# Phase boundaries of a two-layer trunk: single tiles transposed, norms by half rows, other places for the second-half sums

## The chip, the cores and the metric

The kernel runs on one core of one Trainium2 chip. The metric is device time in microseconds (us) of one execution. The kernel before takes 2263.08 us, the median of 3 runs (2262.11 to 2267.9).

## The reference, cut to what matters

The kernel computes two layers of a trunk over 640 tokens of width 1024: 512 sample tokens and 128 prompt tokens, in fp32. Each layer has three sublayers: a gated FFN of inner width 2816, a token mixer (RG-LRU scans in layer 0, window pooling in layer 1) and a second FFN. Each of the three does the same around its core:

```python
h = _modulate(_rmsnorm(x, norm_g[l, 0]), sh1, sc1)
x = x + 0.5 * g1 * _rmsnorm(_swiglu(h, ffn_w1[l, 0], ffn_w3[l, 0], ffn_w2[l, 0]), norm_g[l, 1])
```

So a sublayer needs 1/rms of x per token, a scaling and a shift per column, the core, 1/rms of its result y, and a product with a gate row. The shifts, scales and gates come from a matmul of the conditioning vector with a large weight (the modulation).

## The kernel before, in words

The tokens lie in five tiles of 128: tiles 0 to 3 are the sample, tile 4 the prompt. A row tile `y[t]` or `x` is 128 tokens by 1024. Matmul operands are fp32 numbers split into a high and a low part (`split`: ScalarE copies the high part, L207, VectorE subtracts for the low part, L208), with three matmuls for each product. Weights are split in the same way from a loaded tile `raw` (L136 on ScalarE, L137 on VectorE) and handed out by a generator that makes them ahead as far as a fixed number of buffers allows (`done`, `ahead`).

There are six phases (layer, sublayer): (0,0) FFN, (0,1) RG-LRU, (0,2) FFN, (1,0) FFN, (1,1) pooling, (1,2) FFN. The first products of an FFN go by a seven-product scheme on the token halves of 320 columns: the operands `A11`, `A12` need the first 320 tokens (tiles 0, 1 and half of 2), while `S1` to `S4` and `A22` need the second half too, through sums (`h_sums`, L410 to L413: four VectorE operations and five splits). `ffn_start` (L608) runs four products with `A11` and four with `A12` (96 matmuls of 320 columns, L472), and `seven_rest` then takes `S2`, `S3`, `S1`, `A22` and `S4` (12 matmuls each).

A phase ends in `final` (L575). For each tile it runs the last 24 matmuls of 512 columns (L553), adds them to y in two halves (L561), and then:

- `c_res`: sum of squares of y on ScalarE over 1024 columns (L349), addition of the epsilon on VectorE (L350), power -1/2 on POOL (L352), y times 1/rms times gate row G in one VectorE operation (L376), addition to x (L377).
- `c_next`: the same norm for x (L349, L350, L352), a scaled copy into y on ScalarE (L382), and a store of x to memory (L383).
- `c_h`: for tiles 0 and 1, 2 and 3, and 4 alone, transposes on TensorE (L430), scale and shift on VectorE (L447) and ScalarE (L449), and the splits or sums.

Pairs mean that tiles 0 and 1 are transposed after tile 1's norm, 2 and 3 after tile 3's:

```python
PAIRS = {1: (0, 1), 3: (2, 3), 4: (4,)}
```

Pooling has `pool_start` (L872: mix products, L897) and `pool_rest` (L930), which runs `pool_box` (L907, matmuls L918) for a tile, then `c_res` and `c_next` of it. RG-LRU has `rg_start` (L796) and `rg_rest`.

The modulation is a generator too (`mod_gen`, L262): each step loads 512 KB into one of two buffers `mw` and runs four small matmuls. The two buffers are shared with the x tiles of the final. `mod_step(n)` places n steps at given points of the program, and `mod_until` runs what is left. The gate rows G are made by L304 (TensorE) and L307 (ScalarE) into a single buffer.

The program is handed to a scheduler that fixes the order on each engine from the order of the code and from its own estimates; the order in which an engine works through its queue doesn't change at run time.

## Time and profile before

| | |
|---|---|
| median of 3 runs | 2263.08 us |
| the profiled execution | 2265.16 us, of which 2263.4 are its span |
| TensorE (PE) | 2114.6 us busy, 93% of the span, 13015 matmuls |
| VectorE (DVE) | 1688.3 us, 75% |
| ScalarE (ACT) | 979.9 us, 43% |
| POOL | 78.2 us, 3% |
| memory traffic | 260.40 MB read, 15.74 MB written, 122 GB/s over the span |

The profile names engines PE, PEld (weight loads of PE, beside PE), DVE, ACT, POOL and SP (the queue that issues most DMAs). `L472` is line 472 of the kernel. PEclk is the share of full speed that TensorE's clock was granted; 0.5 is its lower level of 1.2 GHz, 1.0 is 2.4 GHz. Idle time of an engine is listed with what ended it.

### The profile page before, as it was taken

How to read it: one execution, taken by the hardware profiler on the slowest of the kernel's cores; microseconds unless marked ns; L12 is line 12 of the kernel's file. 1: busy time of each engine (PE TensorE's matmuls, PEld its weight loads, DVE VectorE, ACT ScalarE, POOL GpSimd, SP SyncE). 2: the span in 40 equal slices, each digit the busy share in tenths (PEclk: the TensorE clock that was granted, in tenths of full speed). 3: DMA queues.
4: the chain of work that ended last, by engine and by line, in shares of the span. 5: the costliest groups of instructions: out<-in, count | busy, mean ns of one | idle time of the engine just before them, and what ended most of it. 6: DMA issues, size and time to landing. Idle time of an engine off the chain costs nothing.

```text
span 2263.4 us, 32357 instructions
## 1 busy us (share of the span) xinstructions
PE 2114.6 (93%) x13015; PEld 1894.6 (84%) x13015; DVE 1688.3 (75%) x2604; ACT 979.9 (43%) x1555; POOL 78.2 (3%) x107
## 2 busy tenths in 40 slices
PE   6899999997998699999998899999998499999998
PEld 4788889986897588899997788898997389999996
DVE  5967777765988786777776867777777587787875
ACT  5443333355856553333335543332337454333332
POOL 0000000000211100000000000000001000000000
PEclk7999999998999799999999899999999699999999
DMA  8424322235433443322223543344235452222222
GB/s 277 165 98 140 131 103 94 75 112 167 136 112 112 149 173 131 130 98 72 92 75 124 197 149 131 115 147 149 75 103 175 155 174 94 75 91 70 83 75 93
DMA packets 72710, 278.23 MB, mean 123 GB/s; under 512 B 7392, under 2 KB 15600, under 8 KB 61296
## 3 DMA queue, kind: packets, MB, share of 16 engines
q1 hardware_dynamic: 72528, 276.16, 35.2%
q8 instruction: 102, 1.67, 0.3%
q14 instruction: 48, 0.39, 0.1%
q0 software_dynamic: 32, 0.01, 0.0%
HBM read 260.40 MB, written 15.74 MB: 122 GB/s over the span
## 4 chain that ended last, share of the span: by engine, by line
PE 75%; DVE 10%; ACT 6%; DMA 5%; issue 2%; POOL 1%; SPq 1%; POOLq 0%; ACTq 0%; DVEq 0%
PE q L472 43%; PE b L553 24%; PE m L262 2%; PE b L472 2%; DMA mw<-in_mod_w_dram 2%; DMA raw<-in_w_dram 2%; PE q L481 2%; DVE mw L377 2%; POOL st L352 1%; DVE yacc L376 1%; DVE wp L177 1%; DVE h L776 1%; ACT h L738 1%; DVE h L208 1%; DVE wp L137 1%
## 5 line engine op out<-in xcount | busy, mean ns | idle before, releaser
L472 PE MATMUL q<-h,wp 128*128 128x320 f32 x6912 | 1049.7, 312 | 6.0 <-DVE c L504 2.6
L472 PEld LDWEIGHTS q<-h,wp 128*128 128x128 f32 x6912 | 1024.1, 189 | 35.4 <-issue 15.2
L553 PE MATMUL b<-wp,g 128*128 128x512 f32 x2880 | 670.6, 392 | 2.8 <-DVE g L208 2.0
L553 PEld LDWEIGHTS b<-wp,g 128*128 128x128 f32 x2880 | 537.7, 188 | 120.9 <-issue 6.2
L136 ACT ACTIVATE wp<-raw 128x512 fp32r<-128x512 f32 x440 | 267.6, 628 | 636.5 <-PE b L553 294.3
L137 DVE TENSOR_TENSOR wp<-raw,wp 128x512 fp32r<-128x512 f32 x440 | 298.1, 689 | 107.0 <-ACT wp L136 106.2
L561 DVE TENSOR_TENSOR yacc<-yacc,b 128x512 f32<-128x512 f32 x380 | 258.3, 685 | 119.4 <-PE b L553 117.3
L177 DVE TENSOR_TENSOR wp<-raw,wp 128x1024 fp32r<-128x1024 f32 x118 | 144.2, 1223 | 69.7 <-PE q L472 59.5
L174 ACT ACTIVATE wp<-raw 128x1024 fp32r<-128x1024 f32 x94 | 99.6, 1061 | 151.2 <-PE q L472 143.3
L136 ACT ACTIVATE wp<-T 128x512 fp32r<-128x512 f32 x176 | 109.3, 627 | 104.2 <-PE q L472 103.3
L137 DVE TENSOR_TENSOR wp<-T,wp 128x512 fp32r<-128x512 f32 x176 | 118.0, 689 | 14.4 <-ACT wp L136 14.2
L150 DVE TENSOR_TENSOR T<-raw 128x1024 f32<-128x1024 f32 x88 | 107.7, 1224 | 26.7 <-DMA raw<-in_w_dram 25.4
L481 PE MATMUL q<-h,wp 128*128 128x320 f32 x768 | 123.6, 316 | 2.2 <-DVE wp L177 2.2
L481 PEld LDWEIGHTS q<-h,wp 128*128 128x128 f32 x768 | 116.2, 191 | 9.9 <-issue 4.9
L262 PE MATMUL m<-mw,csil 128*32 128x256 f32 x1024 | 85.3, 402 | 23.2 <-DMA mw<-in_mod_w_dram 22.3
L430 PE MATMUL q<-cols,yacc 128*128 128x128 f32 x200 | 38.1, 351 | 67.9 <-ACT yacc L382 67.6
L352 POOL TENSOR_TENSOR st<-st,mhalf 128x1 f32<-128x1 f32 x60 | 43.6, 726 | 1562.1 <-DVE st L350 1553.8
L430 PEld LDWEIGHTS q<-cols,yacc 128*128 128x128 f32 x200 | 30.3, 181 | 78.4 <-ACT yacc L382 78.0
L207 ACT ACTIVATE g<-c 128x1280 fp32r<-128x1280 f32 x44 | 56.2, 1277 | 71.8 <-DVE c L537 71.5
L472 PE MATMUL b<-h,wp 128*128 128x320 f32 x480 | 74.9, 312 | 2.5 <-DVE c L497 1.3
L472 PEld LDWEIGHTS b<-h,wp 128*128 128x128 f32 x480 | 71.1, 188 | 6.1 <-issue 2.5
L208 DVE TENSOR_TENSOR g<-c,g 128x1280 fp32r<-128x1280 f32 x44 | 65.5, 1488 | 10.0 <-ACT g L207 9.7
(184 smaller groups left out, 1584.0 us busy)
## 6 DMA issues: line engine op xcount, KB each, us to landing
raw<-in_w_dram SPq DMA_DIRECT2D x88, 1024.0 KB, 4.8
mw<-in_mod_w_dram SPq DMA_DIRECT2D x130, 512.0 KB, 4.3
raw<-in_w_dram SPq DMA_DIRECT2D x88, 512.0 KB, 4.6
...
wp<-in_mod_w_dram SPq DMA_DIRECT2D x8, 512.0 KB, 10.4
```

The lines of the kernel that those rows point to most:

```text
L136: nc.scalar.activation(w[:, 0:512], src, AF.Copy)
L137: V.tensor_sub(w[:, 512:D], src, w[:, 0:512].bitcast(F32))
L150: V.tensor_sub(T, raw[:, 512:1536], raw[:, 0:1024])
L174: nc.scalar.activation(wh, r, AF.Copy)
L177: V.tensor_sub(wl, r, wh.bitcast(F32))
L208: self.nc.vector.tensor_sub(lo, src, hi.bitcast(F32))
L262: nc.tensor.matmul(ps[32 * j:32 * j + 32, 0:256], self.csil[:, k, :], w[:, j * 256:(j + 1) * 256], start=(k == 0), stop=(k == KC - 1), til ...
L430: nc.tensor.transpose(pt[:, q * w + i * P:q * w + (i + 1) * P], self.y[t][:, (j * n + q) * P:(j * n + q + 1) * P], self.col("ident"))
L472: self.nc.tensor.matmul(out, a, b[:, k], start=(start and not onto and k == first and n == 0), stop=(stop and k == last and n == 2), skip_ ...
L481: self.nc.tensor.matmul(out, a[:, sl], b[k // 2][:, k % 2, cols], start=(n == 0), stop=(n == 3 * KC - 1))
L553: nc.tensor.matmul(pb, a[:, ts_], b[:, ns], start=(c == 0), stop=(c == 3 * len(fl) - 1))
L561: nc.vector.tensor_add(y, y, pb)
```

## The change

1. **Norms by half rows.** `square` takes 512 columns and adds into one of two columns of a statistic; one VectorE operation (L347) adds the two and the epsilon; the power on POOL stays. y times G runs by halves (L379) without 1/rms; then x = y times 1/rms plus x, by halves (L387). The copies to y are by halves too (L399).
2. **`close`**, shared by `final` and pooling, runs product, half norm, product, half norm, and transposes tile t-2 while tile t is under way. Tiles are transposed one at a time into two banks (L476), and tiles 3 and 4 not in `close` at all: `ffn_start` and `rg_start` place them between the first products of the next phase, `pool_start` after the mixes of tiles 0 to 2.
3. **`h_sums`** is a generator: S2 first, the other sums later, with second-half columns in tiles of their own.
4. **Weights and modulation.** `room` keeps six weight buffers free at the start of an FFN and gives them back one per product. `mod_step(5)` and `mod_step(4)` go from `ffn_start`, `mod_step(9)` from `rg_start`.
5. RG-LRU's state transpose moves behind the final, and the second column block's first product starts earlier.

```diff
--- before.py
+++ after.py
...
-        nc.scalar.activation(junk, src, AF.Square, scale=1.0 / 32.0, accum_out=ms)
-        nc.vector.tensor_scalar(ms, ms, EPS, None, op0=ALU.add)
...
+        nc.vector.scalar_tensor_tensor(ms[:, 0:1], ms[:, 0:1], EPS, ms[:, 1:2], op0=ALU.add, op1=ALU.add)
...
+    def square(self, junk, src, ms, n):
+        self.nc.scalar.activation(junk, src, AF.Square, scale=1.0 / 32.0, accum_out=ms[:, n:n + 1])
...
-        rs = self.rstd(y)
...
-        nc.vector.scalar_tensor_tensor(y, y, rs, self.G[(l, s)][:, v], op0=ALU.mult, op1=ALU.mult)
-        nc.vector.tensor_add(x, x, y)
...
+    def res_half(self, t, n, l, s):
+        y = self.y[t][:, n * 512:(n + 1) * 512]
+        self.square(self.t("mhl", [P, 512], BF16), y, self.ms, n)
+        self.nc.vector.tensor_mul(y, y, self.G[(l, s)][:, v, n * 512:(n + 1) * 512])
+    def res_close(self, t):
+        x, y = self.xt[t], self.y[t]
+        rs = self.rstd(self.ms)
+        for n in range(2):
+            ns = slice(n * 512, (n + 1) * 512)
+            self.nc.vector.scalar_tensor_tensor(x[:, ns], y[:, ns], rs, x[:, ns], op0=ALU.mult, op1=ALU.add)
+    def c_next(self, t):
+        x, y = self.xt.pop(t), self.y[t]
+        ms = self.t("st", [P, 2])
+        for n in range(2):
+            ns = slice(n * 512, (n + 1) * 512)
+            self.square(y[:, ns], x[:, ns], ms, n)
+        rs = self.rstd(ms)
+        for n in range(2):
+            ns = slice(n * 512, (n + 1) * 512)
+            self.nc.scalar.activation(y[:, ns], x[:, ns], AF.Copy, scale=rs)
...
+    def h_sums(self, ks, cols, second):
         V = self.nc.vector
+        f21, f22, s1, s2 = second
+        f11, f12 = (x[:, ks, cols] for x in self.F[0])
         V.tensor_add(s1, f21, f22)
+        V.tensor_sub(s2, s1, f11)
+        self.h_put("S2", ks, cols, s2)
+        yield
+        V.tensor_sub(f11, f11, f21)
+        self.h_put("S3", ks, cols, f11)
+        self.h_put("S1", ks, cols, s1)
+        self.h_put("A22", ks, cols, f22)
+        V.tensor_sub(f12, f12, s2)
+        self.h_put("S4", ks, cols, f12)
...
-    def c_h(self, tiles, l, s, plain):
+    def c_t(self, t, l, s, plain, tag="q"):
...
+                if w < P:
+                    tmp = self.t("yacc", [P, D]).rearrange("p (n k t) -> p n k t", n=4, k=HK)
+                    second = [tmp[:, n] for n in range(4)]
+                else:
+                    if t == 3:
+                        self.f2 = [self.t("g", [P, 2 * TOK])[:, 0:D].rearrange("p (k t) -> p k t", k=HK) for _ in range(4)]
+                    o = (t - 3) * P
+                    second = [x[:, :, o:o + P] for x in self.f2]
+                parts.append((slice(a - t * P, P), lambda kk: second[kk // HK][:, kk % HK]))
+                self.sums[t] = self.h_sums(slice(0, HK), slice(a - HT, b - HT), second)
...
+        self.room = max(0, self.room - self.room_step)
+        self.done(1, self.room)
...
+    def close(self, product, l, s, nxt):
         if nxt:
             (self.new_plain if nxt[2] else self.new_h)()
+        self.sums = {}
         for t in range(NT):
+            self.res_open(t)
+            for n in range(2):
+                product(t, n)
+                self.res_half(t, n, l, s)
+            self.res_close(t)
             if nxt:
+                self.c_next(t)
+                if t >= 2:
+                    self.c_t(t - 2, *nxt)
             else:
                 self.store(t)
         self.x_home = self.spill
+        self.g_busy = False
+    def final(self, fl, l, s, nxt, start_next):
+        ws = [self.pair() for _ in fl]
+        self.close(lambda t, n: self.mmB(t, n, fl, ws, False), l, s, nxt)
         self.g.clear()
         if not nxt:
             return
+        start_next(nxt, 2 * len(fl))
...
-    def ffn_start(self, nxt):
+    def ffn_start(self, nxt, used):
         self.mod_allow(self.phase_mods[nxt[0:2]])
         self.ffn_open()
-        for m in range(4):
+        self.room, self.room_step = 6, 0
+        self.done(used, self.room)
+        copy = lambda m: self.nc.scalar.activation(self.s1[m], self.c11[m], AF.Copy)
+        for m in range(2):
             self.prod(self.c11[m], "A11")
-            self.nc.scalar.activation(self.s1[m], self.c11[m], AF.Copy)
-        self.mod_step(5)
-        for m in range(4):
+            copy(m)
+        self.c_t(3, *nxt, tag="b")
+        for m in range(2, 4):
+            self.prod(self.c11[m], "A11")
+            copy(m)
+        for t in (2, 3):
+            next(self.sums[t])
+        for m in range(2):
             self.prod(self.c11[m], "A12", onto=True)
-        self.mod_step(4)
-        self.ahead()
+        self.c_t(4, *nxt, tag="b")
+        next(self.sums[4])
+        for m in range(2, 4):
+            self.prod(self.c11[m], "A12", onto=True)
+        for t in (2, 3, 4):
+            next(self.sums[t], None)
+        self.room_step = 1
...
+        self.done(used, 5)
+        w = [self.pair(), self.pair()]
+        self.rg_xr(0, w[0], 0)
+        self.c_t(3, *nxt, tag="b")
+        self.rg_xr(1, w[1], 0)
+        self.c_t(4, *nxt, tag="b")
         self.rx = [self.t("h", [P, 2 * XW]) for _ in range(6)] + [self.t("c", [P, 2 * XW]) for _ in range(2)]
-        w = self.pair()
-        self.rg_xr(0, w, 0)
-        self.mod_step(9)
-        self.rg_xr(0, w, 1)
+        self.rg_xr(0, w[0], 1)
         self.done(2, 2)
         self.rg_conv(0)
         self.rg_xsplit(0)
+        self.rg_xr(1, w[1], 1)
+        self.done(2, 4)
...
+        self.final((4, 5, 6, 7), l, s, nxt, start_next)
         pt = self.p("m")
         self.nc.tensor.transpose(pt[0:16, 0:P], self.nst, self.col("ident"))
         so = self.t("mrow", [P, P])[0:16]
         self.nc.vector.tensor_copy(so, pt[0:16, 0:P])
         self.nc.gpsimd.dma_start(self.io["out_st"], so)
-        self.final((4, 5, 6, 7), l, s, nxt, start_next)
...
+        for pr in range(2):
+            for t in range(3):
+                mix(t, pr)
+        for t in range(3, NT):
+            self.c_t(t, *nxt)
...
-        self.new_h()
-        for t in range(NT):
-            self.pool_box(t)
-            self.c_res(t, l, s)
-            self.c_next(t, *nxt)
-        self.g_busy = False
-        self.ahead()
-        start_next(nxt)
+        self.close(self.pool_box, l, s, nxt)
+        start_next(nxt, 0)
...
```

TensorE at the boundary from (0,2) to (1,0), before. `yacc_7661` and `yacc_7662` are the rows of tiles 3 and 4, `q_...` the banks, `h_10854` the first operand of the FFN:

```order
L430 MATMUL q_11114<-cols_64,yacc_7661 128x128
L430 MATMUL q_11114<-cols_64,yacc_7660 128x128
L430 MATMUL q_11114<-cols_64,yacc_7661 128x128
L430 MATMUL q_11184<-cols_64,yacc_7662 128x128 x4
L430 MATMUL q_11193<-cols_64,yacc_7662 128x128 x4
L472 MATMUL q_11248<-h_10854,wp_10811 128x320
L472 MATMUL q_11248<-h_10855,wp_10811 128x320
L472 MATMUL q_11248<-h_10854,wp_10811 128x320 x2
```

The last transposes of the pairs and all eight of tile 4 stand ahead of the first FFN product.

TensorE at the same place after the change. `yacc_7736` and `yacc_7737` are tiles 2 and 3; `b_11272` is the last block product:

```order
L580 MATMUL b_11272<-wp_10909,g_10985 128x512
L580 MATMUL b_11272<-wp_10924,g_10984 128x512
L580 MATMUL b_11272<-wp_10909,g_10984 128x512
L476 MATMUL q_11304<-cols_64,yacc_7736 128x128 x4
L476 MATMUL q_11319<-cols_64,yacc_7736 128x128 x4
L476 MATMUL b_11384<-cols_64,yacc_7737 128x128 x4
L476 MATMUL b_11393<-cols_64,yacc_7737 128x128 x4
L498 MATMUL q_11335<-h_10988,wp_10945 128x320
L498 MATMUL q_11336<-h_10988,wp_10962 128x320
L498 MATMUL q_11337<-h_10988,wp_10978 128x320
L262 MATMUL m_11675<-mw_11676,csil_68 32x256
```

The transposes of tiles 2 and 3 stand between the last block product and the first FFN product, and those of tile 4 no longer do. A little further on the same engine, in the first products:

```order
L498 MATMUL q_11336<-h_10990,wp_11360 128x320 x2
L498 MATMUL q_11336<-h_10991,wp_11360 128x320
L498 MATMUL q_11336<-h_10990,wp_11360 128x320
L476 MATMUL b_11477<-cols_64,yacc_7738 128x128 x4
L476 MATMUL b_11486<-cols_64,yacc_7738 128x128 x4
L498 MATMUL q_11337<-h_10990,wp_11376 128x320
L498 MATMUL q_11337<-h_10991,wp_11376 128x320
```

Tile 4 (`yacc_7738`) is transposed here, into banks `b_...`, after 72 of the 96 matmuls of `ffn_start`.

VectorE at that boundary after the change. L588 adds the last half product to tile 4's rows, L379 multiplies by G, L347 sums the statistic, L387 makes x, L482 scales tile 2's half columns, L208 splits them, L137 is a weight difference:

```order
L379 TENSOR_TENSOR yacc_7738<-yacc_7738,G_7964 128x512
L482 TENSOR_SCALAR yacc_11303<-q_11319,ab_8858 128x64
L482 TENSOR_SCALAR c_11003<-q_11319,ab_8858 128x64
L482 TENSOR_SCALAR yacc_11303<-q_11319,ab_8858 128x64
L482 TENSOR_SCALAR c_11003<-q_11319,ab_8858 128x64
L379 TENSOR_TENSOR yacc_7738<-yacc_7738,G_7964 128x512
L347 SCALAR_TENSOR_TENSOR st_11254<-st_11254 128x1
L482 TENSOR_SCALAR yacc_11303<-q_11319,ab_8858 128x64
L387 SCALAR_TENSOR_TENSOR mw_11181<-yacc_7738,st_11290,mw_11181 128x512 x2
L208 TENSOR_TENSOR h_10989<-c_11002,h_10988 128x4x64
L208 TENSOR_TENSOR h_10991<-c_11003,h_10990 128x4x64
L137 TENSOR_TENSOR wp_11340<-raw_10873,wp_11340 128x512
```

The steps of tile 4 and those of tile 2 alternate, and the weight differences start behind the splits of tile 2 (`h_10989`, `h_10991`), which the first FFN products read.

ScalarE at the end of (1,1), before. L926 scales the box products into rows, L307 makes the gate row G, L349 are the sums of squares:

```order
L926 ACTIVATE yacc_11872<-b_16105,cols_64 128x256
L207 ACTIVATE mhl_15756<-mrow_15753 128x256
L926 ACTIVATE yacc_11872<-b_16105,cols_64 128x256
L136 ACTIVATE wp_16174<-raw_15801 128x512
L136 ACTIVATE wp_16177<-T_16171 128x512
L136 ACTIVATE wp_16180<-T_16171 128x512
L307 ACTIVATE G_15759<-m_15760 128x512
L307 ACTIVATE G_15759<-m_15766 128x512
L307 ACTIVATE G_15759<-m_15772 128x512
L307 ACTIVATE G_15759<-m_15778 128x512
L349 ACTIVATE mhl_15861,st_15862<-yacc_11868 128x1024
L349 ACTIVATE yacc_11868,st_15869<-mw_15857 128x1024
```

ScalarE there after the change, where L985 scales the box products and L353 is a square by half rows:

```order
L985 ACTIVATE yacc_12010<-b_16090,cols_64 128x256 x2
L985 ACTIVATE yacc_12011<-b_16139,cols_64 128x256 x2
L207 ACTIVATE mhl_16013<-mrow_16010 128x256
L307 ACTIVATE G_16016<-m_16017 128x512
L307 ACTIVATE G_16016<-m_16023 128x512
L985 ACTIVATE yacc_12012<-b_16194,cols_64 128x256 x2
L307 ACTIVATE G_16016<-m_16029 128x512
L307 ACTIVATE G_16016<-m_16035 128x512
L353 ACTIVATE mhl_16099,st_16089<-yacc_12010 128x512
L353 ACTIVATE mhl_16119,st_16089<-yacc_12010 128x512
L985 ACTIVATE yacc_12013<-b_16271,cols_64 128x256 x2
L136 ACTIVATE wp_16473<-raw_16041 128x512
```

Two of the four parts of G stand ahead of the third tile's box product, and all of them ahead of the squares, which follow for the first tile before the last box products are scaled.

## Rows read from the trace of the kernel before

**Rows 1.** The whole span cut into stages, one line a stage: start and end, length, then busy time (and number of instructions) of the matrix unit PE, its weight loads PEld, DVE, ACT and POOL, then the granted TensorE clock as a share of full speed, the busy share of the DMA engines and GB/s. The stages are: the first boundary, from the end of phase (0,0) to (0,1); the second, from (0,1) to (0,2); the inner blocks of (0,2); the block ahead of the third boundary, in which the final of (0,2) runs; the third boundary, to (1,0); the mix products of (1,1); its box products with the end of that phase. The last line sums the stages of the whole span.

```profile
476.93:526.04 49.11, 35.75 (x171) 28.17 (x169) 36.99 (x55) 28.88 (x46) 7.70 (x10) 0.90 0.45 159
...
762.09:850.67 88.58, 67.49 (x472) 59.70 (x473) 73.63 (x121) 48.50 (x83) 7.22 (x5) 0.87 0.50 177
850.67:1207.83 357.16, 357.16 (x2161) 327.52 (x2158) 263.42 (x395) 128.51 (x196) 0.00 (x0) 1.00 0.29 103
1207.83:1238.90 31.07, 29.99 (x139) 23.87 (x139) 22.06 (x33) 17.61 (x28) 3.85 (x7) 1.00 0.34 114
1238.90:1322.36 83.46, 66.34 (x471) 58.88 (x470) 72.18 (x117) 43.85 (x79) 3.37 (x3) 0.90 0.52 181
...
1721.88:1747.55 25.67, 21.59 (x166) 18.22 (x165) 18.99 (x35) 18.57 (x35) 2.68 (x4) 0.93 0.58 187
1747.55:1819.63 72.08, 33.50 (x216) 25.59 (x215) 43.18 (x73) 39.82 (x75) 6.14 (x10) 0.67 0.50 167
...
sum 2263.40, PE 2114.57 PEld 1894.57 DVE 1688.28 ACT 979.86 POOL 78.19; mean PE 132.16 PEld 118.41 DVE 105.52 ACT 61.24 POOL 4.89
```

**Rows 2.** Timeline of TensorE at the boundary from (0,2) to (1,0): start in us, time, engine, line, what is written and read, shapes, count, and in brackets the idle time ahead with what ended it.

```profile
1246.55 2.82 PE L430 MATMUL q<-cols,yacc 128*128 128x128 f32 x12 [7.21 <-ACT yacc L382]
1256.21 1.97 PE L430 MATMUL q<-cols,yacc 128*128 128x128 f32 x8 [6.83 <-ACT yacc L382]
1257.83 8.49 PE L472 MATMUL q<-h,wp 128*128 128x320 f32 x48
...
1278.39 2.04 PE L472 MATMUL b<-h,wp 128*128 128x320 f32 x12
...
1287.13 0.64 PE L262 MATMUL m<-mw,csil 128*32 128x256 f32 x8
1287.70 4.68 PE L472 MATMUL b<-h,wp 128*128 128x320 f32 x30
```

**Rows 3.** Timeline of VectorE (DVE) in the same stretch, same columns. A line with x2 holds two instructions that follow each other; its time is that of both.

```profile
1240.62 1.22 DVE L377 TENSOR_TENSOR mw<-mw,yacc 128x1024 f32<-128x1024 f32 x1
...
1243.63 1.28 DVE L137 TENSOR_TENSOR wp<-raw,wp 128x512 fp32r<-128x512 f32 x2
...
1248.33 0.34 DVE L447 TENSOR_SCALAR c<-q,ab 128x64 f32<-128x64 f32 x1
1248.59 0.47 DVE L447 TENSOR_SCALAR g<-q,ab 128x192 f32<-128x192 f32 x1
...
1250.88 0.41 DVE L208 TENSOR_TENSOR h<-c,h 128x256 fp32r<-128x256 f32 x1
```

**Rows 4.** Timeline of TensorE at the end of phase (0,1) and the start of (0,2).

```profile
734.33 0.28 PE L865 MATMUL m<-cols,nst 128*16 128x128 f32 x1 [4.79 <-POOL nst L778]
...
772.70 2.82 PE L430 MATMUL q<-cols,yacc 128*128 128x128 f32 x12 [7.60 <-ACT yacc L382]
...
789.23 7.16 PE L472 MATMUL q<-h,wp 128*128 128x320 f32 x36
...
813.80 6.59 PE L472 MATMUL b<-h,wp 128*128 128x320 f32 x43
```

**Rows 5.** Timeline of TensorE at the start of phase (0,1).

```profile
516.93 2.82 PE L430 MATMUL q<-cols,yacc 128*128 128x128 f32 x12 [8.49 <-ACT yacc L382]
...
548.86 1.49 PE L737 MATMUL b<-wp,wp 128*128 128x320 f32 x9
```

**Rows 6.** Timelines of the end of phase (1,1): TensorE first, then ScalarE (ACT), then VectorE.

```profile
1762.12 0.99 PE L262 MATMUL m<-mw,csil 128*32 128x256 f32 x8 [1.69 <-DMA mw<-in_mod_w_dram]
...
1770.96 0.70 PE L304 MATMUL m<-mhl,bsel 128*128 128x256 f32 x4 [1.04 <-DVE mhl L208]
...
1819.63 2.60 PE L472 MATMUL q<-h,wp 128*128 128x320 f32 x14
...
1777.80 0.60 ACT L307 ACTIVATE G<-m 128x512 f32<-128x512 f32 x1 [1.31 <-PE m L304]
...
1780.35 1.28 DVE L376 SCALAR_TENSOR_TENSOR yacc<-yacc,st,G 128x1024 f32<-128x1024 f32 x1 [0.73 <-POOL st L352]
...
1794.04 1.22 DVE L377 TENSOR_TENSOR mw<-mw,yacc 128x1024 f32<-128x1024 f32 x1
...
1803.58 1.22 DVE L377 TENSOR_TENSOR mw<-mw,yacc 128x1024 f32<-128x1024 f32 x1
...
1809.19 1.23 DVE L377 TENSOR_TENSOR mw<-mw,yacc 128x1024 f32<-128x1024 f32 x1
```

**Rows 7.** Timelines of the last tile of all, VectorE first, then ScalarE.

```profile
2254.27 0.68 DVE L561 TENSOR_TENSOR yacc<-yacc,b 128x512 f32<-128x512 f32 x1
2256.25 0.15 DVE L350 TENSOR_SCALAR st<-st 128x1 f32<-128x1 f32 x1 [1.30 <-ACT mhl L349]
2257.13 1.28 DVE L376 SCALAR_TENSOR_TENSOR yacc<-yacc,st,G 128x1024 f32<-128x1024 f32 x1 [0.73 <-POOL st L352]
...
2255.07 1.06 ACT L349 ACTIVATE mhl<-yacc 128x1024 bf16<-128x1024 f32 x1 [4.58 <-DVE yacc L561]
```

**Rows 8.** Timeline of POOL at two of the boundaries: the powers that make 1/rms.

```profile
782.64 3.74 POOL L352 TENSOR_TENSOR st<-st,mhalf 128x1 f32<-128x1 f32 x1 [9.72 <-DVE st L350]
...
1238.24 0.55 POOL L352 TENSOR_TENSOR st<-st,mhalf 128x1 f32<-128x1 f32 x1 [3.53 <-DVE st L350]
1243.86 1.98 POOL L352 TENSOR_TENSOR st<-st,mhalf 128x1 f32<-128x1 f32 x2 [5.07 <-DVE st L350]
```

More of the change, by code (lines that the diff above doesn't have):

```diff
@@ L78 @@
 PB_PER = 5
-PAIRS = {1: (0, 1), 3: (2, 3), 4: (4,)}
 NB = NF // 2
@@ L113, in init_entries @@
         self.wgen = self.weight_gen()
+        self.room = self.room_step = 0
     def load_upto(self, n):
@@ L405, in h_first, with h_put @@
         self.split(hi[:, ks, cols], lo[:, ks, cols], self.F[0][j][:, ks, cols])
-    def h_sums(self, ks, cols):
+    def h_put(self, n, ks, cols, src):
+        hi, lo = self.H[n]
+        self.split(hi[:, ks, cols], lo[:, ks, cols], src)
+    def h_sums(self, ks, cols, second):
         V = self.nc.vector
-        (f11, f12), (f21, f22), s1 = *([x[:, ks, cols] for x in f] for f in self.F), self.fs1[:, ks, cols]
+        f21, f22, s1, s2 = second
+        f11, f12 = (x[:, ks, cols] for x in self.F[0])
@@ new lines, in c_t @@
+        for j in range(2):
+            pt = self.p(tag)
+            for q in range(HK):
+                kk = j * HK + q
+                nc.tensor.transpose(pt[:, q * P:(q + 1) * P], y[:, kk * P:(kk + 1) * P], self.col("ident"))
+            for q in range(HK):
+                kk = j * HK + q
+                for c, dst in parts:
+                    sr = pt[:, q * P:(q + 1) * P][:, c]
+                    if j % 2:
+                        nc.vector.tensor_scalar(dst(kk), sr, ab[:, 1, kk, v:v + 1], ab[:, 0, kk, v:v + 1], op0=ALU.mult, op1=ALU.add)
+                    else:
+                        nc.scalar.activation(dst(kk), sr, AF.Identity, scale=ab[:, 1, kk, v:v + 1], bias=ab[:, 0, kk, v:v + 1])
+            if plain:
+                for k2 in (2 * j, 2 * j + 1):
+                    self.split(self.hh[k2][:, :, sl], self.hl[k2][:, :, sl], hf[:, 2 * k2:2 * k2 + 2])
+            elif t * P < HT:
+                self.h_first(j, slice(0, HK), slice(t * P, min((t + 1) * P, HT)))
@@ L905, in pool01, with pool_box @@
         return self.pb01[b][:, o * P:(o + 1) * P]
[L907 removed]
+    def pool_box(self, t, pr):
         nc = self.nc
         yt = self.y[t]
[L910 to L928 removed]
+        pb = self.p("b")
+        for g in range(2):
+            gg = 2 * pr + g
+            terms = [(self.pwhere[gg, t, j], j) for j in range(NT) if (gg, t, j) in self.pwhere]
+            n = 0
+            for hl in (1, 0):
+                for (bi, j) in terms:
+                    nc.tensor.matmul(pb[:, g * 256:(g + 1) * 256], self.pool01(bi),
+                                     self.qs[j][hl][:, gg * 256:(gg + 1) * 256],
+                                     start=(n == 0), stop=(n == 2 * len(terms) - 1))
+                    n += 1
+        for g in range(2):
+            gg = 2 * pr + g
+            dst, src, ic = yt[:, gg * 256:(gg + 1) * 256], pb[:, g * 256:(g + 1) * 256], self.col("icnt", gg * NT + t, 1)
+            if pr == 0:
+                nc.scalar.activation(dst, src, AF.Copy, scale=ic)
+            else:
+                nc.vector.tensor_scalar(dst, src, ic, None, op0=ALU.mult)
     def pool_rest(self, l, s, nxt, start_next):
@@ L971, in start @@
         self.new_h()
+        self.F[1] = [self.view(self.t("g", [P, 2 * TOK])) for _ in range(2)]
+        places = [self.view(self.t("g", [P, 2 * TOK])), None]
         for t in range(NT):
-            rs = self.rstd(self.y[t], self.t("T", [P, D], BF16))
+            ms = self.t("st", [P, 2])
+            for n in range(2):
+                ns = slice(n * 512, (n + 1) * 512)
+                self.square(self.t("T", [P, D], BF16)[:, 0:512], self.y[t][:, ns], ms, n)
+            rs = self.rstd(ms)
             nc.scalar.activation(self.y[t], self.y[t], AF.Copy, scale=rs)
@@ L1018, in mod @@
             if r >= 2:
-                self.h_sums(h_k, slice(0, HT))
+                if r == 2:
+                    places[1] = self.view(self.t("g", [P, 2 * TOK]))
+                for _ in self.h_sums(h_k, slice(0, HT), [x[:, h_k] for x in self.F[1] + places]):
+                    pass
         self.ffn_open_start()
```

159 lines of the change are left out of this document (44 added, 115 removed).

## The prediction

> **What bounds the kernel now.** I read the stage windows first [rows 1]. Inside a phase TensorE never stops: 357.16 of 357.16 us in the longest of them, at full clock. Over the span it is busy 2114.57 of 2263.40 us, so 148.8 us are idle, and they lie at the phase boundaries: 13.4 us at the first (476.93 to 526.04), 21.1 at the second (762.09), 17.1 at the third (1238.90), 4.1 and 38.6 around the pooling. The rest is the start, the tail and short waits. The change leaves TensorE's work as it was (200 transposes before and after, the same products), so what it can win is this idle time, and the lower clock after it: granted 0.90 in the third boundary, 0.67 in the pooling. The time of the profiled execution is 2265.16 us, 1.8 more than its span and 2.1 above the median of the runs; I sum against the former and take 2.1 off at the end.
>
> Next the timelines of the boundary from FFN to FFN. TensorE waits 7.21 us for the scaled copy of tile 3, transposes tiles 2 and 3 as a pair, waits 6.83 for tile 4, and starts the first product at 1257.83, 18.9 us after the last product of the old phase [rows 2]. VectorE works almost without a stop meanwhile (72.18 of 83.46 us, [rows 1]): weight differences in two and three at a time stand between the steps of the last tile [rows 3]. So the boundary is a chain through VectorE's queue, of which TensorE needs for its first products only tiles 0, 1 and half of 2.
>
> **The third boundary, FFN to FFN.** T0 is the end of the last block product. In the new order VectorE has after T0, up to the last operand of the first product: an addition of 512 columns 0.68 and a statistic 0.15 (both as in [rows 7]), two products with G 1.28 (the price of two 512 steps in a row), eight small scalings of 64 columns that start 0.26 apart 2.0, the pair that makes x 1.28 (an estimate: the old step of 1024 columns in [rows 7] takes as long), and two splits at 0.42 [rows 3]: 6.2 us. A power on POOL, 0.55 [rows 8], and its handing over add about 0.9, and the transposes of tile 2 start at once. I take T0+8. What held the first product up, the last two tiles, comes later: tile 3's transposes stand ahead of the products, tile 4's after 72 of them. The 96 products at 0.156 (4.68 for 30, [rows 2]) are 15.0, the eight transposes and a low clock at the start some 2 more (the 48 now at 8.49 are already 1.0 over that rate): T0+25. Now the sums are late: some 30 VectorE instructions, the weight differences among them, stand before the low half of S2, 17.7 us by the same durations, so S2 starts at T0+27.7 and waits about 2; S3's low half is ready at about T0+33, a second wait of 3.5. Forty-eight products follow, 7.5: T0+40.5. Before, the same point is 1287.70 plus 18 x 0.156, which is T0+51.6. Of these 11.1 us the modulation matmuls taken out must be paid later: 64 stood there, eight of which put the next product off by 0.57 [rows 2], 4.6 us; about half to all of them move. Gain 6.5 to 8.6; I take **7**. Ends: 2, if both late sums wait three us longer; 11, if neither waits.
>
> Halving costs little by the trace: one step of 1024 columns takes 1.22, two of 512 in a row 1.28 [rows 3], so 0.06 more per pair. The Trainium skill ("VectorE: DVE Perf Modes", "The TRN2 errata") speaks against the halving: a fixed latency per instruction, (N+151)/0.96 ns for an fp32 operation of two tensors, with advice for 512 elements or more. By that a pair costs 0.157 more, not 0.06; over 60 pairs it would be 9.4 us instead of 3.6 on VectorE, nearly all beside TensorE, and some 2 us of the sum. The trace's pair overlaps where the rule adds up; the measurement decides.
>
> **The second, RG-LRU to FFN.** The same chain. Before, the first product begins at 789.23, 27.1 after the window's start, behind a wait of 7.60 for tile 3 among others, and the fifth of the products in question ends with 38 of the 43 that start at 813.80 [rows 4], at about T0+57.5. With T0+40.5 that is 17. Less 3.4 for 48 modulation matmuls that move, less 2 because VectorE is fuller here (73.63 us busy, [rows 1]), less 3 because the nine modulation steps that stood at this phase's start are now made up at its end, where each needs a load into two buffers. I take **8.5**; ends 0 (the loads cost 10) and 14. The state's transpose leaves the front of the final; but the wait of 4.79 there [rows 4] ends on POOL's copy of the state, and the operand of the products behind it comes out of the same chain of work, so I count nothing; were it all the transpose's, 4.8 more.
>
> **The first, FFN to RG-LRU.** Of 13.4 us idle [rows 1] the wait for tile 3 is 8.49 [rows 5]. The chain to the first product stays as above, with 5 to 7 us of wait. Gain **7**, ends 2 and 10. The first gate product, 548.86 now, shows it.
>
> **The pooling, both ends.** 97.75 us between the phases, 42.7 of them idle [rows 1]. Before, modulation loads end with the matmul at 1762.12; its row then stands on VectorE behind other work, the four parts of G run alone from 1770.96 to 1778.4 [rows 6], and only at 1780.35 is the first tile multiplied. In the new order these parts stand among the box products and ScalarE makes G ahead of the squares: first use about 1771, 9 us earlier. The loads themselves start some us earlier, since the last tile frees its buffer sooner; they are eight in a row through two buffers, so I count 2. The five tiles then follow one another; the last two additions to x stand 9.5 and 5.6 us behind those before them, and I keep the whole stretch as it is. From the last addition at 1809.19 to the first product at 1819.63 are 10.4 us; by the chain above it is about 3, of which the late sums take 4 back: 3. Together **14**. Ends: -5, if a long spacing like the 9.5 comes four times more (4 x 3.9 = 15.6 lost) and the sums wait 3 longer; 25, if the long one goes too and the sums don't wait.
>
> **The tail.** After the last product come 0.68, a square of 1.06, the power, and the two steps of 1024 columns, 1.28 [rows 7] and 1.22 as in [rows 3]. The first half's square and product with G go under the last products; a pair of 1.28 replaces 1.28 and 1.22. Gain **1.5**, ends 0.5 and 2.5. Start and inner blocks: 0, since there TensorE has no idle time to give and its work is the same; the modulation steps put into them are the ones already subtracted.
>
> Sum 7 + 8.5 + 7 + 14 + 1.5 = 38. 2265.2 - 38 - 2.1 = 2225.
>
> **Rivals.** (a) VectorE sets the boundaries. It is busy 72 of 83 us at the third and 74 of 89 at the second, its work is not reduced, and at the end of a phase it will need about 6.5 us a tile (three pairs at 1.28, four scalings, two splits, by [rows 3]) against TensorE's 6.2 (a fifth of the 31.07 us ahead of the third boundary, [rows 1]). If its backlog at T0 grows by what was saved, half of each gain is left: 3.5 + 4 + 3.5 + 7 + 1.5 = 19.5, 2243. For it: how little VectorE rests there. Against: room for weights is held back, so fewer differences stand in the queue.
> (b) The waits nearly vanish: gains at their upper ends, 10 + 14 + 11 + 25 + 2 = 62, 2201. For it: at no boundary is TensorE's own work the limit. Against: the two late sums above.
> (c) Slower: POOL's power is held up by a denser VectorE. It takes 0.55 when VectorE waits, but two took 1.98 and one 3.74 while VectorE ran without a stop [rows 8]. In the new order VectorE has fewer gaps. Two powers per tile at the three boundaries' last tile and ten in the pooling are on the path, 16. At 3.2 more each that is 51 against a gain of 38: 2276. It turns to slower from 2.4 us each. Against: most waits for the power leave VectorE idle, which makes it fast again.
> The Trainium skill ("GPSIMD Engine Reference", "Key points") says that GpSimd shares its interface with VectorE instructions of two inputs in SBUF, the ones in question; the trace agrees with 0.55 against 3.74.
> (d) The change gives nothing: what is late now, modulation loads and VectorE, is late again by as much: 2259 to 2266.
>
> **Numbers.** Forecast 0.52 (2212 to 2237), (a) 0.20, (b) 0.14, (c) 0.08, (d) 0.06. A measurement tells 0.3%, 7 us, from no change: faster 0.86, same 0.06, slower 0.08. The ends of the five terms lie 5, 8.5, 5, 19 and 1 below what I took; they hardly come together, and their squares add to some 22. Upwards (a) is inside with 2250; downwards I go to 2206, which leaves about half of (b) out and (c) and (d): 2 in 10 in all.
>
> **What would show it.** TensorE's first product 8 us after the last block product at the second and third boundary, with a gap of 2 and one of 3 to 4 before S2 and S3. G's four parts among the box products, and the last addition to x 11 us sooner than now, counted from the pooling's first product. TensorE idle near 112 instead of 148.8. The power on POOL at 0.55 to 1. I am wrong if VectorE is still busy with weights when the last tile's statistic is ready, if modulation loads stop TensorE at the end of the RG-LRU phase for more than 3 us, or if the pooling tiles come at 7.5 us or more apart.

## The result and the profile after

The changed kernel takes 2239.65 us (2235.2 to 2242.64, 4 runs) against 2262.6 of the kernel before in the same comparisons: a ratio of 0.9896, 95% interval 0.9869 to 0.9923. Its profiled execution takes 2239.14 us, 26.0 less than the one before; the span fell from 2263.4 to 2236.9. TensorE is idle for 119.4 us (2236.9 less 2117.5 busy) instead of 148.8. The two profiles lie 3 us further apart than the medians, whose difference is 23.0.

To see where the 26.5 us of span come from, I took from both traces the starts and ends of the products of 512 columns. A *start* lasts from the last such product of a phase to the first of the next FFN, *inner* from there to the last block's first product. The last column is the gain.

| stretch | before | after | gain |
|---|---|---|---|
| up to the last block of (0,0) | 476.93 | 474.65 | 2.3 |
| last block of (0,0), then (0,1) to its end | 285.16 | 273.56 | 11.6 |
| start of (0,2) | 88.58 | 81.22 | 7.4 |
| inner (0,2) | 356.97 | 361.28 | -4.3 |
| last block of (0,2), start of (1,0) | 114.65 | 111.53 | 3.1 |
| inner (1,0) | 368.26 | 374.74 | -6.5 |
| last block of (1,0), pooling, start of (1,2) | 185.73 | 170.75 | 15.0 |
| inner (1,2) | 348.12 | 351.17 | -3.1 |
| last block of (1,2) and the tail | 39.00 | 38.00 | 1.0 |

The first row is no part of the change: with start-up code alike in all kernels but for the norms, it lay between 472.4 and 476.9 in the runs of this study.

The stage windows of after, which answer to [rows 1] (same columns), for the starts and inner stretches of (0,2) and (1,0):

```profile
748.21:829.43 81.22, 67.56 (x426) 60.39 (x424) 73.02 (x136) 47.79 (x99) 4.44 (x5) 0.87 0.51 179
829.43:1190.71 361.28, 361.28 (x2206) 329.04 (x2205) 265.02 (x397) 131.16 (x201) 0.00 (x0) 1.00 0.30 104
1220.72:1302.24 81.52, 66.85 (x425) 59.15 (x425) 73.67 (x137) 47.19 (x99) 3.96 (x4) 0.90 0.53 178
1302.24:1676.98 374.74, 374.40 (x2342) 333.92 (x2341) 268.40 (x406) 131.59 (x200) 0.00 (x0) 1.00 0.36 124
```

The starts are VectorE's (DVE, third busy time): 73 of 81 us, and the inner stretches TensorE's. In the start of (1,0) VectorE's waits come to 7.5 us, of which 0.7 end on TensorE; before, 6.5 of 10.8 did. TensorE has 425 matmuls there where it had 469, and the stretch is hardly shorter.

TensorE at the third boundary, which answers to [rows 2]; the old phase ends at 1220.72:

```profile
1228.38 1.97 PE L476 MATMUL b<-cols,yacc 128*128 128x128 f32 x8 [6.12 <-ACT yacc L399]
1231.08 1.17 PE L498 MATMUL q<-h,wp 128*128 128x320 f32 x3 [0.73 <-ACT h L207]
1232.69 1.06 PE L262 MATMUL m<-mw,csil 128*32 128x256 f32 x2 [0.45 <-DMA mw<-in_mod_w_dram]
1233.68 11.80 PE L498 MATMUL q<-h,wp 128*128 128x320 f32 x69
...
1246.12 3.74 PE L498 MATMUL q<-h,wp 128*128 128x320 f32 x24
...
1251.66 0.41 PE L498 MATMUL b<-h,wp 128*128 128x320 f32 x1 [0.81 <-ACT h L207]
1253.96 1.06 PE L262 MATMUL m<-mw,csil 128*32 128x256 f32 x2 [1.88 <-DMA mw<-in_mod_w_dram]
...
1267.28 2.04 PE L498 MATMUL b<-h,wp 128*128 128x320 f32 x12
```

Three products start 10.4 us after the old phase (before: 18.5, from the end of its last product at 1239.35; the prediction's 18.9 counts from 1238.90), the rest after 13.0. The 96 matmuls of `ffn_start` end at 1249.86, the five products with the sums (60 matmuls into banks `b`) at 1269.32. VectorE there, in the place of [rows 3]:

```profile
1224.19 1.41 DVE L387 SCALAR_TENSOR_TENSOR mw<-yacc,st,mw 128x512 f32<-128x512 f32 x2 [0.44 <-POOL st L349]
1225.53 0.68 DVE L208 TENSOR_TENSOR h<-c,h 128x512 fp32r<-128x512 f32 x1
1226.13 0.68 DVE L588 TENSOR_TENSOR yacc<-yacc,b 128x512 f32<-128x512 f32 x1
...
1231.07 1.42 DVE L387 SCALAR_TENSOR_TENSOR mw<-yacc,st,mw 128x512 f32<-128x512 f32 x2 [0.47 <-POOL st L349]
1232.40 0.75 DVE L208 TENSOR_TENSOR h<-c,h 128x256 fp32r<-128x256 f32 x2
```

Tile 4's last addition (L588) runs 5.4 us after the last product: tile 3's x (L387), which waits for its power, and a split of tile 1 stand ahead of it. Tile 2's splits, which the products need, stand behind tile 4's x.

The end of the pooling, in the place of [rows 6]; its phase begins at 1707.36:

```profile
1752.81 0.73 PE L304 MATMUL m<-mhl,bsel 128*128 128x256 f32 x4
...
1754.92 1.34 DVE L379 TENSOR_TENSOR yacc<-yacc,G 128x512 f32<-128x512 f32 x2
...
1757.06 1.42 DVE L387 SCALAR_TENSOR_TENSOR mw<-yacc,st,mw 128x512 f32<-128x512 f32 x2 [0.33 <-POOL st L349]
...
1768.41 3.20 POOL L349 TENSOR_TENSOR st<-st,mhalf 128x1 f32<-128x1 f32 x1 [3.19 <-DVE st L347]
...
1772.42 1.97 PE L476 MATMUL q<-cols,yacc 128*128 128x128 f32 x8 [9.93 <-ACT yacc L399]
...
1787.73 11.80 PE L498 MATMUL q<-h,wp 128*128 128x320 f32 x72
...
1788.65 1.41 DVE L387 SCALAR_TENSOR_TENSOR mw<-yacc,st,mw 128x512 f32<-128x512 f32 x2 [0.44 <-POOL st L349]
```

The last part of G stands among the box products, and the first product with G comes 47.6 us after the phase's begin (before 58.3, 1780.35 less 1722.04, the end of the last product of (1,0)). The first FFN product comes after 80.4 us instead of 97.6. The five additions to x lie further apart than they did: from the first to the last are 31.6 us (1757.06 to 1788.65); before they were 26.5, from the line below to 1809.19 in [rows 6]:

```profile
1782.68 1.22 DVE L377 TENSOR_TENSOR mw<-mw,yacc 128x1024 f32<-128x1024 f32 x1
```

### The profile page after: what moved, and what is told of

Same layout as the page of the kernel before. It is cut to its first block, busy times and chain, and to the rows that moved or that the text cites. A ratio compares the mean times of both kernels' runs of the same rounds, so it can differ in the third digit from the quotient of the medians.

```text
span 2236.9 us, 32742 instructions
## 1 busy us (share of the span) xinstructions
PE 2117.5 (95%) x13015; PEld 1897.3 (85%) x13015; DVE 1701.5 (76%) x2753; ACT 1012.9 (45%) x1779; POOL 73.2 (3%) x107
## 4 chain that ended last, share of the span: by engine, by line
PE 77%; DVE 10%; ACT 5%; DMA 4%; issue 2%; POOL 1%; SPq 1%; POOLq 0%; DVEq 0%; ACTq 0%
PE q L498 43%; PE b L580 24%; PE m L262 3%; PE q L507 2%; PE b L498 2%; DMA mw<-in_mod_w_dram 2%; DVE mw L387 1%; DMA raw<-in_w_dram 1%; POOL st L349 1%; DVE wp L177 1%; DVE wp L137 1%; DVE h L208 1%; ACT yacc L399 1%; ACT mhl L353 1%; DVE h L824 1%
## 5 line engine op out<-in xcount | busy, mean ns | idle before, releaser
L137 DVE TENSOR_TENSOR wp<-raw,wp 128x512 fp32r<-128x512 f32 x440 | 298.2, 688 | 115.5 <-ACT wp L136 114.0
L588 DVE TENSOR_TENSOR yacc<-yacc,b 128x512 f32<-128x512 f32 x380 | 258.6, 685 | 125.2 <-PE b L580 122.6
L137 DVE TENSOR_TENSOR wp<-T,wp 128x512 fp32r<-128x512 f32 x176 | 118.5, 689 | 15.1 <-ACT wp L136 14.9
L262 PE MATMUL m<-mw,csil 128*32 128x256 f32 x1024 | 87.6, 393 | 13.9 <-DMA mw<-in_mod_w_dram 12.2
L349 POOL TENSOR_TENSOR st<-st,mhalf 128x1 f32<-128x1 f32 x60 | 40.0, 666 | 1558.2 <-DVE st L347 1549.7
L498 PEld LDWEIGHTS b<-h,wp 128*128 128x128 f32 x480 | 76.1, 201 | 15.6 <-ACT h L207 5.2
L498 PE MATMUL b<-h,wp 128*128 128x320 f32 x480 | 81.7, 327 | 7.1 <-ACT h L207 3.3
L208 DVE TENSOR_TENSOR g<-c,g 128x1280 fp32r<-128x1280 f32 x44 | 65.5, 1488 | 8.9 <-ACT g L207 8.5
L558 ACT ACTIVATE c<-c 128x960 f32<-128x960 f32 x44 | 43.9, 998 | 57.0 <-DVE c L536 57.0
L262 PEld LDWEIGHTS m<-mw,csil 128*32 128x32 f32 x1024 | 27.8, 109 | 46.3 <-issue 20.5
```

Source lines behind the costliest of these rows:

```text
L137: V.tensor_sub(w[:, 512:D], src, w[:, 0:512].bitcast(F32))
L208: self.nc.vector.tensor_sub(lo, src, hi.bitcast(F32))
L262: nc.tensor.matmul(ps[32 * j:32 * j + 32, 0:256], self.csil[:, k, :], w[:, j * 256:(j + 1) * 256], start=(k == 0), stop=(k == KC - 1), til ...
L349: nc.gpsimd.tensor_tensor(rs, ms[:, 0:1], self.mhalf, op=ALU.pow)
L498: self.nc.tensor.matmul(out, a, b[:, k], start=(start and not onto and k == first and n == 0), stop=(stop and k == last and n == 2), skip_ ...
L588: nc.vector.tensor_add(y, y, pb)
```

## The experiments

All stretches as in the first table; "RG" is from the last product of (0,0) to the last of (0,1), "pool" from the last product of (1,0) to the first block of (1,2).

| kernel | ratio to before, interval | RG | start (0,2) | inner (0,2) | start (1,0) | inner (1,0) | pool | inner (1,2) |
|---|---|---|---|---|---|---|---|---|
| before | | 253.65 | 88.58 | 356.97 | 82.94 | 368.26 | 154.25 | 348.12 |
| after | 0.9896, 0.9869 to 0.9923 | 243.58 | 81.22 | 361.28 | 81.52 | 374.74 | 140.37 | 351.17 |
| e1 | 0.9868, 0.9847 to 0.9890 | 243.85 | 81.92 | 356.47 | 81.07 | 368.24 | 144.51 | 348.84 |
| e2 | 0.9998, 0.9986 to 1.0010 | 253.18 | 83.08 | 362.71 | 76.09 | 374.99 | 149.42 | 349.58 |
| e3 | 0.9928, 0.9902 to 0.9955 | 246.07 | 77.36 | 361.29 | 79.47 | 374.86 | 145.53 | 350.24 |
| e4 | 0.9975, 0.9961 to 0.9990 | 243.79 | 85.38 | 361.27 | 84.27 | 374.23 | 146.86 | 350.61 |
| f1 | 1.0094, 1.0079 to 1.0109 | 253.58 | 88.55 | 357.00 | 89.70 | 368.24 | 159.89 | 347.67 |
| f2 | 0.9933, 0.9913 to 0.9953 | 243.56 | 77.37 | 361.82 | 84.35 | 374.13 | 142.68 | 350.23 |
| f3 | 0.9969, 0.9957 to 0.9981 | 242.91 | 81.78 | 362.07 | 80.05 | 374.13 | 145.43 | 350.94 |
| f4 | 0.9889, 0.9873 to 0.9905 | 243.53 | 80.51 | 356.50 | 81.28 | 368.24 | 148.28 | 351.27 |
| g1 | 0.9859, 0.9839 to 0.9879 | 243.82 | 76.12 | 361.28 | 73.31 | 374.95 | 138.44 | 350.23 |
| g2 | 0.9989, 0.9980 to 0.9998 | 251.25 | 87.51 | 357.71 | 79.48 | 368.25 | 152.72 | 347.67 |
| g3 | 0.9925, 0.9901 to 0.9949 | 247.28 | 79.50 | 362.61 | 80.65 | 374.25 | 140.72 | 351.43 |
| g4 | 0.9893, 0.9876 to 0.9909 | 247.83 | 79.53 | 356.61 | 79.75 | 368.27 | 142.47 | 348.72 |

Where the code is the same, inner stretches repeat within 1.3 us, starts within 3.5 (g3's start of (1,0) has after's code and is 0.9 shorter, its start of (0,2) 1.7; g2's start of (1,0) has before's and is 3.5 shorter), and pool within 8 (f4's has after's code and is 7.9 longer), so I read single profiles for differences above that, and the ratios for whole times. The kernel before took 2256.9 to 2262.6 us in the four comparisons, and after ran in the first of them alone, so a time that is expected below is best compared by the ratio too.

**Where do the modulation steps belong?** e1 puts them back into the FFN starts of after; e2 takes them out of before.

```diff
             self.prod(self.c11[m], "A11")
             copy(m)
+        self.mod_step(5)
...
             self.prod(self.c11[m], "A12", onto=True)
+        self.mod_step(4)
```

> The changed kernel (2239.65 us) with the modulation steps put back into the start of each FFN: five after the products with A11, four after those with A12. Theory A (VectorE sets these boundaries, so TensorE had time there for the modulation matmuls and has none in the inner blocks): the three inner stretches of (0,2), (1,0), (1,2) fall from 361.3, 374.7, 351.2 us back to about 357, 368, 348, 14 us in all, and the three starts grow by at most 4 in all: 2226 to 2231. Theory B (the matmuls cost the same wherever they stand, the third boundary lost by the late addition of tile 4 alone): the starts grow by 3 to 5 each: 2237 to 2242.

> The kernel before (2262.6 us) without its nine modulation steps in the start of each FFN, which then run later; nothing else is changed. Theory A: the starts stay within 2 us of 88.6, 82.9 and 56.7 us and the inner stretches grow by 4 to 6 each, together 2270 to 2276. Theory B: what the starts lose the inner stretches gain, 2261 to 2265.

The two agree with different theories. In after the steps cost 4.8 and 6.5 us of the inner stretches and, put back, at most 0.7 of the starts of (0,2) and (1,0) (2.3 less in the inner stretch of (1,2), 4.1 more in the pool, which is within its spread). The time is 2231.05 us, the lowest of a complete version here, though its interval overlaps after's. In before, the starts gave up 5.5 and 6.9 us and the inner stretches took 5.7 and 6.7: nothing won. There, once the first product of the third boundary runs, TensorE is the limit. Timeline of TensorE in e2, from that product on: 144 matmuls without a wait.

```profile
1252.81 1.97 PE L430 MATMUL q<-cols,yacc 128*128 128x128 f32 x8 [6.83 <-ACT yacc L382]
1254.43 15.32 PE L472 MATMUL q<-h,wp 128*128 128x320 f32 x96
1269.59 7.23 PE L472 MATMUL b<-h,wp 128*128 128x320 f32 x48
```

**Does VectorE's work set the new starts?** e4 adds to it, g1 takes away.

```diff
         self.c_t(3, *nxt, tag="b")
+        junk = self.t("mhl", [P, 512])
+        for _ in range(8):
+            self.nc.vector.tensor_sub(junk, self.cols[:, 0:512], self.cols[:, 32:544])
```

> The changed kernel with eight more VectorE operations of 512 columns (4.8 us) at the start of each FFN, whose results nothing reads. Theory A: all three boundaries grow by 3.5 to 4.8 us: 2250 to 2254. If waits for ScalarE, POOL and loads set the boundaries and VectorE has gaps for it: at most 4 us in all, 2239 to 2244.

```diff
-                V.tensor_sub(w[:, 512:D], src, w[:, 0:512].bitcast(F32))
+                if self.lean:
+                    nc.scalar.activation(w[:, 512:D], src, AF.Copy)
+                else:
+                    V.tensor_sub(w[:, 512:D], src, w[:, 0:512].bitcast(F32))
```

> The changed kernel, in which the low parts of the eight to ten weights made during the start of an FFN are a plain copy on ScalarE instead of a subtraction on VectorE: it leaves the low parts of those weights out of the result, and takes 5 to 6 us from VectorE in each start. Theory A (VectorE's work sets the starts): the starts of (0,2) and (1,0), 81.2 and 81.5 us, shrink by 3 to 5 each, in all 2226 to 2232. If waits for loads or ScalarE set them: within 1.5 us each, 2236 to 2242.

The start windows, e4's two and then g1's two, columns as in [rows 1]:

```profile
748.26:833.64 85.38, 67.05 (x426) 60.44 (x424) 77.01 (x143) 48.00 (x99) 5.30 (x5) 0.86 0.49 165
1224.94:1309.21 84.27, 67.97 (x425) 59.32 (x425) 78.01 (x145) 47.50 (x99) 5.16 (x4) 0.88 0.51 172
```

```profile
750.41:826.53 76.12, 64.64 (x426) 57.58 (x424) 66.58 (x125) 52.14 (x109) 3.04 (x5) 0.89 0.51 185
1217.84:1291.15 73.31, 62.54 (x426) 55.58 (x425) 67.19 (x126) 51.47 (x109) 2.80 (x4) 0.93 0.55 192
```

With 4.0 and 4.3 us more of VectorE the starts grew by 4.2 and 2.8; with 6.4 and 6.5 less they shrank by 5.1 and 8.2. VectorE's work sets them, roughly one for one: e4's growth is near what starts spread by, but its whole time, 0.9975 against 0.9896, is longer clear of the intervals, and g1's shortening is above the spread. g1, at 2226.38 us, leaves work out and is no version to use.

**Does it matter when the first product starts?** e3 moves it forward, f3 back.

```diff
+            if nxt and t >= 2:
+                self.c_t(t - 2, *nxt)
             self.res_close(t)
             if nxt:
                 self.c_next(t)
-                if t >= 2:
-                    self.c_t(t - 2, *nxt)
```

> The changed kernel with one line moved: tile t-2 is transposed ahead of the second half of tile t's norm instead of behind it, so that tile 2's splits stand on VectorE ahead of tile 4's norm. Theory B: the first products of the second and third boundary start 3 to 4 us sooner after the last block product (now 13 us to the first full run) and the sums with them: 2229 to 2235. Theory A: VectorE has the same work up to S4, so the products start sooner and wait longer for S2 and S3: 2237 to 2241.

f3 does the same with `t - 1` ahead of an FFN and has no `c_t(3, ...)` in `ffn_start`.

> The changed kernel, in which ahead of an FFN tile t-1 and not t-2 is transposed while tile t is under way, ahead of its norm, so that tile 3 too is done in the close of the old phase. If VectorE's work behind the last block product sets the start (theory A), the starts of (0,2) and (1,0) shrink by 2 to 4 us each, the finals grow by under 1: 2231 to 2236. If TensorE then waits for the copies inside the final, each final grows by 2 to 4 and the time stays at 2238 to 2243.

First products 6.2 and 7.3 us after the old phase (e3), 8.5 and 10.4 (after), 19.1 and 17.1 (f3: TensorE waits 11.47 us for a copy); starts of 77.4 and 79.5, 81.2 and 81.5, 81.8 and 80.1. TensorE at the third boundary, e3 (the old phase ends at 1217.11) and then f3 (1222.27):

```profile
1239.53 3.74 PE L498 MATMUL q<-h,wp 128*128 128x320 f32 x24
...
1262.99 2.04 PE L498 MATMUL b<-h,wp 128*128 128x320 f32 x12
```

```profile
1237.77 1.97 PE L476 MATMUL q<-cols,yacc 128*128 128x128 f32 x8 [11.47 <-ACT yacc L399]
...
1252.54 3.74 PE L498 MATMUL q<-h,wp 128*128 128x320 f32 x24
...
1268.84 2.04 PE L498 MATMUL b<-h,wp 128*128 128x320 f32 x12
```

The 96 matmuls end 26.2 us after the old phase in e3, 29.1 in after and 34.0 in f3; the five with the sums end at 47.9, 48.6 and 48.6. At the second boundary the difference does not vanish so soon (the five end at 46.7, 44.8 and 50.1), but f3's start is 0.6 us longer there with a first product that comes 10.6 later. e3 wins 3.9 and 2.0 in the two starts, little more than they spread by, and loses 2.5 in RG, and its ratio doesn't tell it from after.

f3 isn't the late product alone: it also does tile 3's work ahead of the last product. Its starts didn't shrink as theory A expected; the finals ahead of them changed by -0.6 and +1.2, so what was taken out was made up by TensorE's longer wait. Its time, 2250.40 us, is above both expectations, and by the ratio longer than after's clear of the intervals. Its profile is of its fastest execution (2243.12), in which the pool is 5.1 longer, so where the rest goes isn't shown.

**What are the half rows worth?** f1 is before with them alone, f2 is after without them.

```diff
-            self.mmB(t, 0, fl, ws, False)
-            self.mmB(t, 1, fl, ws, False)
-            self.c_res(t, l, s)
+            self.res_open(t)
+            for n in range(2):
+                self.mmB(t, n, fl, ws, False)
+                self.res_half(t, n, l, s)
+            self.res_close(t)
```

> The kernel before with the norms by half rows and nothing else of the change (pairs of tiles, places and modulation steps as before). Theory H (the half rows bring the gain at the RG-LRU and pooling boundaries): from the end of (0,0) to the end of (0,1) 253.7 us falls by 3 or more, from the end of (1,0) to the first block of (1,2) 154.3 falls by 5 or more: about 2250. Theory T (the places of the transposes and of G bring it): both fall by under 2, about 2258 to 2262.

> The changed kernel with the norms by whole rows as before (1/rms and G in one operation of 1024, x added in a second one), all else changed. Theory H: 8 us or more are lost, 2247 to 2255. Theory T: at most 3 us, 2239 to 2243.

By the stretches theory H falls: f1's RG is before's and its pool 5.6 us longer, where 3 and 5 were to be won, and f2's RG is after's. The whole time is less sharp: f2 has after's median (2239.85) and span (2236.8), but a ratio of 0.9933 against 0.9896; the intervals overlap, and a gain of some us isn't ruled out. Two things that half rows do are seen in both kernels. The tail is 38.0 us with them (after, f1) and 38.9 to 39.0 without (f2, before). The five additions to x in the pooling span 31.6 and 37.5 us with them (after, f1) and 26.1 and 26.5 without (f2, before): there they cost some 5 us of the tiles' chain.

f1 is 0.9% slower, and at its third boundary not because halves are dear. Timeline of TensorE there:

```profile
1249.41 2.82 PE L446 MATMUL q<-cols,yacc 128*128 128x128 f32 x12 [8.25 <-ACT yacc L399]
1253.34 1.08 PE L262 MATMUL m<-mw,csil 128*32 128x256 f32 x8 [1.10 <-DMA mw<-in_mod_w_dram]
1258.00 1.08 PE L262 MATMUL m<-mw,csil 128*32 128x256 f32 x8 [3.58 <-DMA mw<-in_mod_w_dram]
1263.29 1.08 PE L262 MATMUL m<-mw,csil 128*32 128x256 f32 x8 [4.21 <-DMA mw<-in_mod_w_dram]
1267.26 1.11 PE L446 MATMUL q<-cols,yacc 128*128 128x128 f32 x4 [2.89 <-ACT yacc L399]
```

The scheduler put three modulation matmul groups, each waiting for its load, ahead of tile 4's transposes; the first product started 31 us after the old phase. Here an edit changed the order elsewhere, and that set the time of this start, 6.8 us more.

**RG.** g2 moves the state's transpose behind the final in before; g3 puts `mod_step(9)` back into `rg_start` of after.

```diff
+        self.final((4, 5, 6, 7), l, s, nxt, start_next)
         pt = self.p("m")
...
-        self.final((4, 5, 6, 7), l, s, nxt, start_next)
```

> The kernel before with the transpose of RG-LRU's state moved behind the final, nothing else. Theory N (the wait of 4.79 us ahead of the final was the state's): the stretch from the end of (0,0) to the end of (0,1), 253.7 us, falls by 3.5 to 5, 2255 to 2259 against 2259 to 2263. Theory O (the final's own operand was as late, as I had taken it): under 1 us.

> The changed kernel with the nine modulation steps put back into the start of RG-LRU. If their old place cost TensorE time there (part of the gain of 10 us between the end of (0,0) and the end of (0,1) is their move): the stretch of 243.6 us grows by 2 to 4. If they are hidden at either place: within 1 us.

g2 wins 2.4 us of 253.65, between the two theories; in place of the 4.79 TensorE now waits 2.76 and 1.62 for the final's own operand:

```profile
729.54 2.35 PE L553 MATMUL b<-wp,g 128*128 128x512 f32 x9 [2.76 <-DVE g L208]
733.50 10.95 PE L553 MATMUL b<-wp,g 128*128 128x512 f32 x47 [1.62 <-DVE g L208]
```

g3 loses 3.7 of the 10.1 that RG gained. If the two add, 4 are left, which were not taken apart.

**Two tries for a better version.** f4 has e1's steps except in (1,2), and e3's order in the finals ahead of an FFN. g4 is e1 with `if j % 2 and tag != "b":` for VectorE's scalings, so ScalarE scales tiles 3 and 4.

> The changed kernel with the modulation steps put back in the starts of (0,2) and (1,0) but not of (1,2), and with tile t-2 transposed ahead of tile t's norm in the finals that lead to an FFN, not elsewhere. Both alone gave 4.1 and 6.9 us, and 3.9 and 2.1 us, in the stretches of (0,2) and (1,0). If they add: 17 us below the changed kernel, 2222. If VectorE's work sets the start (theory A), steps and earlier products share one gain: 2226 to 2229.

> The changed kernel with all modulation steps put back into the FFN starts, as in e1 (0.9868 of before), and with tiles 3 and 4 scaled and shifted by ScalarE alone (VectorE has eight operations less, 2.6 us, in each start). Theory A: 2 us less at each start than e1: ratio 0.983 to 0.986. If ScalarE's queue is as late as VectorE's: as e1, 0.986 to 0.989.

f4 keeps e1's inner stretches, but its two starts, 80.5 and 81.3, are e1's and not e3's: the gains don't add, as theory A has it. Its time, 2232.5 us, is above both expectations, with a pool 7.9 longer than after's. g4's starts shrink by 2.4 and 1.3 against e1, near the 2 expected but within what starts spread by; RG grows by 4.0 (its tiles 3 and 4 are changed too), and the ratio doesn't tell it from e1 or after.

## Why the prediction was right or wrong

Direction and range were right; the number, 2225, was 14.6 us low. The time lies nearest to rival (a), 2243. The range, which had been drawn up to 2250 to hold that rival, held because of it: VectorE does set the second and third boundary. The sum hides larger errors than its own: these two boundaries gave 15.8 us less than forecast, the first gave 4.6 more, and in the pooling two errors cancelled, which is luck.

- **Third boundary, forecast +7: wrong, -3.4** (3.1 with the last block, less 6.5). The step that failed is the chain itself: "Forty-eight products follow, 7.5: T0+40.5". I took TensorE's products for the pace once the sums were made. The five products ended at T0+48.6, and 4.1 of these 8.1 us were there when the 96 ended, at T0+29.1 and not T0+25. VectorE's remaining work is the pace up to the next block (e4, g1): the 11.1 us that the chain took off would have left 71.8 of 82.9 us, and VectorE had 71.7 us of work there before. The change gives it more: 73.67 us and 137 instructions against 71.66 and 117 in before, and 69.82 and 114 in e2, where the modulation matmuls are out as well. "An addition of 512 columns" right after T0 was also wrong: tile 3's norm stands ahead of it by 5.4 us. But e3 and f3 show that this cost little: 0.7 us or nothing by the end of the five products. As g2 has 3.5 us less than before in this start with the same code, the 3.1 may be nothing at all.
- **Modulation steps, "about half to all of them move".** Mis-sized: I took 4 and 3.4 us off for (1,0) and (0,2), and nothing for (1,2). They cost 6.5, 4.3 and 3.1, so 6.5 of the miss is theirs, and e1 gets 13.6 of the 13.9 back. Out of each start of (0,2) and (1,0) went 32 modulation matmuls and the gates' own products (L304), 16 a phase, which I had not counted.
- **Second boundary, +8.5: 3.1** (7.4 less 4.3); e4 and g1 show the same cause. **First, +7: 11.6 with RG's end**, of which g2 shows 2.4 for the transpose that I counted at nothing, and g3 3.7 for the steps, which I had taken as a loss of 3. The two terms together were 15.5, measured 14.7. (The first line of [rows 1] begins with the last block of (0,0), not behind it; 12.5 of its 13.4 us idle lie behind that block's end at 508.44.)
- **Pooling, 14: 11.9** (15.0 less 3.1). G came 10.8 us sooner, as forecast (9 and 2). The rest agrees by luck. I kept the stretch of the five tiles as it was, and it grew by 5.1; two of the four spacings are 8.2 and 9.9, beyond the 7.5 that I had named as a sign of being wrong, and the last addition to x came 5.9 us sooner, not 11. From that addition to the first block, where I took 3, 8.0 were won (59.1 against 67.1). One power took 3.20 us on the path.
- **Tail, 1.5: 1.0.** The pair that makes x takes 1.41, not the 1.28 I had estimated.
- Rival (c) didn't come: the mean power fell, 666 ns against 726 (40.0 us for 60), though single ones took up to 3.20. Rival (d) didn't either.
- Halving: x's pair costs 0.13 more than the one step of 1024 (1.41 against 1.28), y times G, the one time its halves follow each other, 0.12 (1.34 against 1.22), twice the 0.06 I took. The rule of the Trainium skill ("VectorE: DVE Perf Modes", "The TRN2 errata"), which is for an operation of two tensors, gave an estimate of 0.157, somewhat above both.
